# Loading two rows of the first tile ahead, in four transfers of some of the partitions

## The chip, the cores and the metric

The kernel runs on one core of a Trainium2 chip. The metric is the device time of one execution in microseconds (us); lower is better. Times are the median of several unprofiled runs; one more execution is taken with the hardware profiler, and all durations come from it.

## The reference

```python
def reference(x):                      # x: (32, 512, 2048) float32
    half_dim = x.shape[-1] // 2
    x1, x2 = x[..., :half_dim], x[..., half_dim:]
    silu_x1 = x1 * (1 / (1 + np.exp(-x1)))
    return (silu_x1 * x2).astype(np.float32)      # (32, 512, 1024)
```

Each row of 2048 numbers is cut in two halves; the silu of the first is multiplied with the second. 134.22 MB are read and 67.11 MB are written, so the work is mostly moving data.

## The kernel before

The 16,384 rows are cut into 16 tiles of 1024 rows. A tile lies on 128 partitions with `K = 8` rows on each; these eight rows are neighbours in the memory, so that one partition's share of a tile is one stretch of 64 KB of the input and one of 32 KB of the output. There are two input buffers (`xt0`, `xt1`) and two output buffers (`ot0`, `ot1`), used in turn by even and odd tiles.

Per tile there are four kinds of work. `load(i)` (L64) issues the transfer of the tile into its buffer from SP's queue. `silu(i, a, b)` (L71) computes the silu of the first half of rows a to b on ACT, in place. `mul(i, a, b)` (L79) multiplies with the second half on DVE and writes the output buffer. `store(i, a, b)` (L90) issues the transfer to the output from ACT's queue. The order is written out by hand (`manual_schedule`), the waits follow from what reads and writes which buffer, and `implied` (L57) drops those that another wait already covers.

The order (L93 to L114): SP issues the loads of tiles 0 and 1 at once. Tile 0 is computed in four pieces of two rows (`FIRST`), and stored in five transfers (`OPENING`, L16), each of some of the partitions: every fourth partition's rows 0 and 1; the partitions halfway between these, rows 0 to 3, then 4 to 7; every fourth partition's rows 2 to 7; and the odd partitions with all rows. Then SP issues the load of tile 2. Tiles 1 to 14 are computed whole and stored whole; as soon as a tile's product is done, its input buffer is free and SP issues the load of the tile two further on. Tile 15 is computed and stored in two halves (`LAST`). At the end SP waits for all stores.

SP thus issues 16 transfers, all loads, and ACT 21, all stores (five of tile 0, fourteen whole ones, two halves). A load waits for the product of the tile that used its buffer before; a store for its product; a product also for the store that last read its output buffer.

What each engine of the chip's transfer hardware does is kept in the trace as packet records: one record for each stretch of memory moved by one of the core's 16 DMA engines, with its start, duration and size. In this kernel a load gives each engine eight packets of 64 KB, and a whole store eight of 32 KB. A further record of 4 bytes on each engine ends each transfer.

Of the kernel before, what the change touches and what calls it, by code (L numbers as in the profile page):

```python
# [1 line left out]

# [4 lines left out]


K = 8

FIRST = [(0, 2), (2, 4), (4, 6), (6, 8)]

LAST = [(0, 4), (4, 8)]


OPENING = [  # L16
    (slice(0, None, 4), slice(0, 2)),
    (slice(2, None, 4), slice(0, 4)),
    (slice(2, None, 4), slice(4, None)),
    (slice(0, None, 4), slice(2, None)),  # L20
    (slice(1, None, 2), slice(None)),
]
SYNC = mybir.DependencyInfo(mybir.DependencyClass.Sync, mybir.DependencyReason.DATA)


@with_exitstack
def kernel(
    ctx: ExitStack,
    tc: tile.TileContext,
    x: bass.AP,  # L30
    out: bass.AP,
):
    nc = tc.nc
    P = nc.NUM_PARTITIONS

    x_flat = x.flatten_outer_dims()
    out_flat = out.flatten_outer_dims()
    num_rows, in_cols = x_flat.shape
    half = in_cols // 2
    dt = x_flat.dtype  # L40
    n_tiles = num_rows // (P * K)
    assert n_tiles * P * K == num_rows

    x_view = x_flat.rearrange("(n p k) d -> n p k d", p=P, k=K)
    out_view = out_flat.rearrange("(n p k) d -> n p k d", p=P, k=K)

    in_pool = ctx.enter_context(tc.tile_pool(name="in_pool", bufs=1))
    out_pool = ctx.enter_context(tc.tile_pool(name="out_pool", bufs=1))
    xts = [in_pool.tile([P, K, in_cols], dt, name=f"xt{j}") for j in range(2)]
    ots = [out_pool.tile([P, K, half], dt, name=f"ot{j}") for j in range(2)]  # L50

    ctx.enter_context(tc.manual_schedule())

    dmas = []
    loads, silus, muls = {}, {}, {}

    def implied(ins, others):  # L57

        for other in others:
            tc.declare_no_dep(ins.ins, other.ins, reason="another wait implies it")

    def load(i):  # L64
        ins = nc.sync.dma_start(out=xts[i % 2], in_=x_view[i])  # L65
        dmas.append(ins)
        loads[i] = ins
        if i >= 2:
            implied(ins, [loads[i - 2], *silus[i - 2]])

    def silu(i, a, b):  # L71
        x1 = xts[i % 2][:, a:b, :half]
        ins = nc.scalar.activation(out=x1, in_=x1, func=mybir.ActivationFunctionType.Silu)  # L73
        silus.setdefault(i, []).append(ins)
        if i >= 2:
            implied(ins, [*silus[i - 2], *muls[i - 2]])
        return ins

    def mul(i, a, b):  # L79
        xt = xts[i % 2]  # L80
        ins = nc.vector.tensor_mul(  # L81
            out=ots[i % 2][:, a:b], in0=xt[:, a:b, :half], in1=xt[:, a:b, half:]
        )
        muls.setdefault(i, []).append(ins)
        implied(ins, [loads[i]])
        if i >= 2:
            implied(ins, [loads[i - 2], *silus[i - 2], *muls[i - 2]])
        return ins

    def store(i, a, b):  # L90
        dmas.append(nc.scalar.dma_start(out=out_view[i][:, a:b], in_=ots[i % 2][:, a:b]))

    load(0)  # L93
    load(1)
    for a, b in FIRST:
        silu(0, a, b)
        mul(0, a, b)
    for ps, ks in OPENING:
        dmas.append(nc.scalar.dma_start(out=out_view[0][ps, ks], in_=ots[0][ps, ks]))
    load(2)  # L100

    for i in range(1, n_tiles - 1):
        silu(i, 0, K)
        mul(i, 0, K)
        store(i, 0, K)
        if i + 2 < n_tiles:
            load(i + 2)

    i = n_tiles - 1
    for a, b in LAST:  # L110
        last_silu = silu(i, a, b)
        last_mul = mul(i, a, b)
    for a, b in LAST:
        store(i, a, b)  # L114


    for group in ([last_silu], [*dmas[-12:-1], last_mul]):
        seen = nc.sync.nop()
        for ins in group:
            tc.add_manual_dep(seen.ins, ins.ins.name, SYNC, reason="the closing waits")  # L120


# [1 line left out]
_INS = ['x']  # L124
_OUTS = [((32, 512, 1024), 'float32')]


# [23 lines left out]
```

## Time and profile before

| what | value |
|---|---|
| median of three unprofiled runs | 470.75 us (470.7 to 471.8) |
| the profiled execution, in all | 472.5 us |
| its span, first to last recorded work | 470.6 us |
| DVE busy | 139.4 us, 20 instructions |
| ACT busy | 114.1 us, 21 instructions |
| read and written | 134.22 MB and 67.11 MB |
| mean rate over the span | 428 GB/s |
| silu of a whole tile, product of a whole tile | 7.03 us, 8.69 us |
| silu and product of two rows of tile 0 | 1.89 us, 2.29 us |
| a load, from its issue to its landing (median) | 41.9 us |
| a whole store, from its issue to its landing (median) | 49.2 us |

The chain of waits is read backwards from the last instruction: at each step it goes to what released the work. It alternates here between products and transfers. A load and a store of two tiles are under way at most times, so the time from issue to landing holds the wait behind earlier packets on the same 16 engines; the rate says how well the engines are used, the landing time doesn't.

This is the opening of the profiled execution in the timeline (start, duration in us, engine, line, operation, count, and in brackets the idle time before and what ended it):

```profile
0.73 115.68 SPq L65 DMA_DIRECT2D xt<-in_x_dram  x6
22.80 5.51 ACT L73 ACTIVATE xt<-xt 128x2048 f32<-128x2048 f32 x3 [20.80 <-DMA xt<-in_x_dram]
24.74 8.90 DVE L81 TENSOR_TENSOR ot<-xt 128x2048 f32<-128x2048 f32 x4 [24.74 <-ACT xt L73]
27.07 0.55 ACTq L99 DMA_DIRECT2D out_dram<-ot  x1
28.22 1.89 ACT L73 ACTIVATE xt<-xt 128x2048 f32<-128x2048 f32 x1
29.27 6.28 ACTq L99 DMA_DIRECT2D out_dram<-ot  x4
```

ACT waits 20.80 us for tile 0, then computes its four silus one after the other; DVE follows a piece behind; the five opening stores are issued from 27.07 to 35.55. A queue's line in this view (SPq, ACTq) gives the time from the first to the last of the merged issues, not work.

### The profile page before, as it was taken

What the parts mean: (1) busy time and instruction counts of PE and PEld (TensorE: products, weight loads), DVE (VectorE), ACT (ScalarE), POOL (GpSimd) and SP (SyncE); (2) the same over time, 40 slices, a digit from 0 to 9 for tenths busy, and PEclk for the clock granted to TensorE, in tenths of its full rate; (3) what the DMA queues carried; (4) which work ended last, traced back from release to release, by engine and by line L of the source; (5) the groups of instructions that cost most, each with busy time, mean ns of one, the idle gap of its engine ahead of it and who ended that gap; (6) DMA issues with size and microseconds to landing.
All of it is one profiled execution on the core that took longest, in us unless ns stands there. A gap on an engine that the chain in (4) does not pass through costs nothing.

```text
span 470.6 us, 169 instructions
## 1 busy us (share of the span) xinstructions
DVE 139.4 (30%) x20; ACT 114.1 (24%) x21; POOL 0.2 (0%) x4
## 2 busy tenths in 40 slices
DVE  0070513307043070420705106061150602507061
ACT  1051405041050501405014050230503205032060
POOL 0000000000000000000000000000000000000000
DMA  8999899999999999999999999999999999999997
GB/s 357 446 462 422 361 484 407 457 432 401 446 454 437 401 448 421 468 401 446 409 440 443 443 407 485 446 393 415 485 404 446 404 443 446 423 429 482 401 407 315
DMA packets 4880, 201.33 MB, mean 428 GB/s; under 512 B 592, under 2 KB 592, under 8 KB 592
## 3 DMA queue, kind: packets, MB, share of 16 engines
q1 hardware_dynamic: 2304, 134.22, 66.1%
q10 hardware_dynamic: 2576, 67.11, 33.1%
HBM read 134.22 MB, written 67.11 MB: 428 GB/s over the span
## 4 chain that ended last, share of the span: by engine, by line
DMA 80%; DVE 14%; ACT 2%; DVEq 1%; issue 0%; SPq 0%
DMA out_dram<-ot 62%; DMA xt<-in_x_dram 18%; DVE ot L81 14%; ACT xt L73 2%; DVEq L146 1%; SPq L65 0%; DVEq L81 0%
## 5 line engine op out<-in xcount | busy, mean ns | idle before, releaser
L81 DVE TENSOR_TENSOR ot<-xt 128x8192 f32<-128x8192 f32 (+2 forms) x20 | 139.4, 6984 | 321.1 <-DMA out_dram<-ot 261.3
L73 ACT ACTIVATE xt<-xt 128x8192 f32<-128x8192 f32 (+2 forms) x20 | 112.8, 5661 | 340.3 <-DMA xt<-in_x_dram 340.3
L73 ACT ACT_TABLE_LOAD x1 | 1.3, 1283 | 0.7 <-PEq L135 0.7
L135 POOL MEMSET const-bfloat16-1.0<- 128x1 bf16 x1 | 0.1, 101 | 0.0
L135 POOL MEMSET const-uint8-127<- 128x1 uint8 x1 | 0.1, 101 | 0.0
L135 POOL MEMSET const-float32-0.0<- 128x1 f32 x1 | 0.1, 98 | 0.2 <-issue 0.2
L135 POOL MEMSET const-float32-1.0<- 128x1 f32 x1 | 0.1, 98 | 0.0
## 6 DMA issues: line engine op xcount, KB each, us to landing
out_dram<-ot ACTq DMA_DIRECT2D x14, 4096.0 KB, 49.2
out_dram<-ot ACTq DMA_DIRECT2D x3, 2048.0 KB, 9.4
out_dram<-ot ACTq DMA_DIRECT2D x2, 512.0 KB, 18.3
out_dram<-ot ACTq DMA_DIRECT2D x1, 768.0 KB, 29.6
xt<-in_x_dram SPq DMA_DIRECT2D x16, 41.9
out_dram<-ot ACTq DMA_DIRECT2D x1, 256.0 KB, 11.0
```

Of the source, the lines that this page charges most:

```text
L73: ins = nc.scalar.activation(out=x1, in_=x1, func=mybir.ActivationFunctionType.Silu)
L81: ins = nc.vector.tensor_mul(out=ots[i % 2][:, a:b], in0=xt[:, a:b, :half], in1=xt[:, a:b, half:])
L135: nc = _bacc.Bacc("TRN2", target_bir_lowering=False, num_devices=1)
L146: with _tile.TileContext(nc) as tc:
```

## The change

Tile 0 is no longer loaded in one transfer. `load` walks a list, `ARRIVING`, when `i == 0`: rows 6 and 7 come first, in four transfers of 16, 16, 32 and 64 partitions (every 8th from 0; every 8th from 4, halfway between; every 4th from 2; the odd ones); then rows 0 to 5 of all 128 partitions in one. All five go out from SP ahead of the load of tile 1. The other tiles are loaded as before. `loads[i]` becomes a list, and the calls of `implied` are adapted to it. The first three silus of tile 0 read rows 0 to 5 and depend on the fifth transfer, the last one on the four others too.

```diff
+ARRIVING = [
+    (slice(0, None, 8), slice(6, None)),
+    (slice(4, None, 8), slice(6, None)),
+    (slice(2, None, 4), slice(6, None)),
+    (slice(1, None, 2), slice(6, None)),
+    (slice(None), slice(0, 6)),
+]
...
     def load(i):
-        ins = nc.sync.dma_start(out=xts[i % 2], in_=x_view[i])
-        dmas.append(ins)
-        loads[i] = ins
-        if i >= 2:
-            implied(ins, [loads[i - 2], *silus[i - 2]])
+        for ps, ks in ARRIVING if i == 0 else [(slice(None), slice(None))]:
+            ins = nc.sync.dma_start(out=xts[i % 2][ps, ks], in_=x_view[i][ps, ks])
+            dmas.append(ins)
+            loads.setdefault(i, []).append(ins)
+            if i >= 2:
+                implied(ins, [*loads[i - 2], *silus[i - 2]])
...
-        implied(ins, [loads[i]])
+        implied(ins, loads[i])
         if i >= 2:
-            implied(ins, [loads[i - 2], *silus[i - 2], *muls[i - 2]])
+            implied(ins, [*loads[i - 2], *silus[i - 2], *muls[i - 2]])
```

A count of the instructions in their order on each engine shows SP with 20 transfers instead of 16 (16x4096 twice, 32x4096, 64x4096, 128x12288, then the whole tiles), and all else in the same order. The eight completion counters that the transfers share in turn are dealt out differently, which adds waits on SP: ahead of the load of tile 2 for the second small transfer, and ahead of the load of tile 4 for the other four parts of tile 0 and for one opening store.

## The prediction

> **What bounds the kernel now.** I read the page's traffic first, then its chain of waits, then the windows view by stage, then the packet records of the trace.
>
> ```profile
> DVE 139.4 (30%) x20; ACT 114.1 (24%) x21; POOL 0.2 (0%) x4
> ...
> HBM read 134.22 MB, written 67.11 MB: 428 GB/s over the span
> ...
> DMA 80%; DVE 14%; ACT 2%; DVEq 1%; issue 0%; SPq 0%
> ```
>
> DVE works 139 us and ACT 114 us of 470.6, so neither sets the end; the chain gives 80% to transfers. The question is how near the 16 DMA engines are to their own limit, and where they fall short of it. The windows (stretch, DVE, ACT and POOL busy, clock, then the DMA share and GB/s, which count a packet where it begins):
>
> ```profile
> 1.73:2.09 0.36, 0.00 (x0) 0.28 (x1) 0.00 (x0) 1.00 7.60 2549
> 2.09:2.45 0.36, 0.00 (x0) 0.00 (x0) 0.00 (x0) 1.00 0.00 0
> 2.45:2.80 0.35, 0.00 (x0) 0.00 (x0) 0.00 (x0) 1.00 0.94 374
> 11.20:28.90 17.70, 4.16 (x2) 6.10 (x4) 0.00 (x0) 1.00 0.96 415
> 28.90:60.90 32.00, 13.43 (x4) 8.24 (x2) 0.00 (x0) 1.00 1.01 424
> 60.90:118.90 58.00, 17.38 (x2) 14.06 (x2) 0.00 (x0) 1.00 1.00 434
> 118.90:176.90 58.00, 17.38 (x2) 14.06 (x2) 0.00 (x0) 1.00 1.00 434
> 176.90:466.90 290.00, 86.99 (x11) 70.39 (x11) 0.00 (x0) 1.00 1.00 433
> 466.20:467.40 1.20, 0.00 (x0) 0.00 (x0) 0.00 (x0) 1.00 0.96 410
> 467.40:468.20 0.80, 0.00 (x0) 0.00 (x0) 0.00 (x0) 1.00 0.06 21
> 468.20:469.50 1.30, 0.00 (x0) 0.00 (x0) 0.00 (x0) 1.00 0.06 25
> ```
>
> From 61 us on the rate is flat at 433 to 434 GB/s with all engines busy. In the packet records each 64 KB packet there takes 2.418 us, and the next begins 2.414 us after it: 65,536 B / 2.414 us x 16 = 434 GB/s. Pure transfer is therefore 201.33 MB / 434 GB/s = 463.9 us, and the span holds only 6.7 us more. Those lie at the two ends. At the start, 2549 GB/s x 0.36 us is 14 packets of 64 KB, and the other two engines' first packets (374 x 0.35 = 2 packets) begin 0.4 to 1.0 us later. At the end, the last three rows hold about 16 KB begun in 0.8 us and 32 KB in 1.3 us: one engine alone is still working. By the packet records fifteen engines end at 467.4 to 467.7 us and one at 469.5: a lag of 1.8 us that the whole kernel waits for.
>
> The same records tell when that lag arises. The odd engine is the one that begins last, at 2.75 us. Against the latest of the others it is 0.28 us behind after its first packet (5.52 against 5.24), still 0.28 when tile 0 has landed (22.43 against 22.15), 0.67 at 41.3, and 1.78 at 61.0; from there on it keeps pace exactly. So it is not a slower engine: its lag is made in the opening, and since no engine is ever idle again, nothing takes it back.
>
> **The change, part by part.** The profiled execution took 472.5 us in all, its span 470.6; the unprofiled runs have their median at 470.75. I work in changes of the span and put them on the median.
>
> *Packets and completions.* Each engine now moves tile 0 in 1+1+2+4 packets of 16 KB and 8 of 48 KB, 16 instead of 8. In the last stores 16 KB packets begin 0.607 us apart, four of them 2.428 against 2.414 for 64 KB: 5 ns a packet, so 8 x 5 = 0.04 us. Each transfer also ends with a 4-byte completion record of 9 ns on each engine: 4 x 9 = 0.04. Together +0.08 us, on the path, as the engines are never idle.
>
> *Issue on SP.* Four more transfers go out ahead of both big loads. A load's issue takes 0.33 to 0.43 us; ACT's issues of every second or fourth partition 0.48 to 0.68. At 0.55 each the fifth issue starts at 0.73 + 4 x 0.55 = 2.9 us and the second tile's at 3.4. An engine's first packet came 1.0 us after the issue (2.0 on the odd engine), so the fifth transfer is ready by 4.9. The eight small packets keep an engine busy to 1.74 + 0.6 (what its first packet took beyond 2.4) + 8 x 0.607 = 7.2 us: cover 2.3 us, price nothing. If that cover failed, each restart would cost the 0.6 us seen on the first packet, 4 x 0.6 = 2.4.
>
> *Compute of tile 0.* The first silu now waits for the fifth transfer, which is the last of the tile as before; the fourth takes four more waits, long fulfilled, some 17 ns each on ACT. That is hidden behind DVE, whose four products take 2.29 each against 1.89 for the silus. What is late next would be the load of tile 2, queued on SP behind the fourth product and issued at 33.67. The tile 1 packets ahead of it run to about 43.4, so the opening's compute has 43.4 - 33.7 - 1.0 = 8.7 us to spare. New waits ahead of SP's loads of tiles 2 and 4 are for transfers landed tens of us earlier; behind them only later loads are queued. Zero.
>
> *The start of the odd engine.* No row shows a transfer with one packet per engine issued to idle queues. If the late beginning comes from handing out 128 rows, a first transfer of 16 rows removes it, and with it the 0.28 us left after the first packet; the most it could bring is the 0.77 to 1.0 us by which the engine starts behind the fourteen. If it belongs to the engine, it brings 0. The other bound is each small transfer restarting like the first one, 0.6 each. I take -0.28: the start's scatter is nearest to hand-out, since the same engine keeps full pace from 61 us on.
>
> *What the lag grows by.* Between 28.9 and 55 us, while the opening stores go out, 64 KB packets take longer than 2.418 us: on a typical one of the fifteen by 0.13 + 0.34 + 0.07 + 0.20 + 0.25 = 1.0 us, on the odd one by 0.21 + 0.49 + 0.34 + 0.51 + 0.45 + 0.30 = 2.3. The two 0.5 us ones are loads that run while the others store. In step with the others it should stretch as they do, and the lag grew by 1.78 - 0.28 = 1.5: I take -1.5. Bounds: -1.5, and +1.5 if new scatter puts another engine as far behind again.
>
> Sum: 0.08 - 0.28 - 1.5 = -1.7 us; 470.75 - 1.7 = **469.05 us** (case A).
>
> [...]
>
> **The rivals.** B: the lag stays. The first packet already absorbs most of the late start (1.0 us at its beginning, 0.28 at its end), and the rest is made by the opening stores, which the change leaves alone. Then only the 0.08 us is added: 470.85. For it: another engine that began 0.77 us late had caught up after one packet. Against: the engine that fell back is the one that started last.
>
> C, the other side: transfers of some of the partitions disturb the stream by themselves. The stretching lies just where the five such stores run, and nowhere after; at the ends of the first three, the next 64 KB packet took about 0.34, 0.20 and 0.25 us longer on the fifteen, up to 0.5 on the odd one. Four such loads at 0.4 are +1.6, the old lag stays, +0.08: 472.4. It decides from about 0.35 us per transfer. Against it: the last two of the five stores, and the boundary between the first two loads, show no stretch.
>
> [...]
>
> **How the numbers follow.** A difference under 0.3%, 1.4 us, is about what a measurement of this kernel can't tell from none: faster is below 469.3, slower above 472.2. Chances: A 0.40 (468.5 to 470.0; 0.35 of it clear of the bound), B 0.24, C 0.20, D 0.16. Faster: 0.35 from A and 0.02 from B. Same: 0.05 from A, 0.19 from B, 0.03 from C, 0.06 from D = 0.33. Slower: 0.03 from B, 0.17 from C, 0.10 from D = 0.30. The range reaches from A's low end (all of the lag and some of the first packet's 0.6) past C: 468.5 to 472.6. A's own is 468.5 to 470.0.
>
> **What would show it.** Right: first packets of all 16 engines within 0.4 us, the last rows of the windows empty after 467.7, the opening row (28.90 to 60.90) nearer 434 GB/s, silu 0 starting within 0.5 us of 22.8. Wrong: one or more engines ending alone as before (B); longer packets before 12 us (C, D: in D about 1.2 us for 16 KB in the first two transfers); a gap in the packets of an engine between 2 and 8 us (the cover on SP failed).

## The result, and the profile after

The changed kernel takes 472.75 us (median of 7 runs, 472.39 to 473.14), the kernel before 470.77 (7 runs, 470.70 to 472.11): ratio 1.0036, 95% interval 1.0026 to 1.0046. It is slower by 2.0 us, where 1.7 us faster was forecast; the time lies just above the range.

The runs come with their spans, and these put the base right. In the comparisons below, where every run is listed with its span, the kernel before was run 79 times. 59 of these runs have a span of at most 469.1 us (mostly 468.8) and a time about 1.9 us above it; 20 have spans of 469.3 to 471.2. The first profile, with its span of 470.6 and 472.5 us in all, was one of the long executions. The changed kernel's profile has a span of 471.0 and 472.75 us in all, its usual time. So the fair comparison is 468.8 with 471.0, not 470.6 with 471.0.

The page of the changed kernel, traffic and the chain's shares by engine:

```profile
HBM read 134.22 MB, written 67.11 MB: 427 GB/s over the span
...
DMA 80%; DVE 14%; ACT 2%; DVEq 1%; SPq 1%; issue 0%
```

Nothing new bounds the kernel; the rate is 1 GB/s lower. Its windows, in the columns of the prediction:

```profile
1.73:2.09 0.36, 0.00 (x0) 0.28 (x1) 0.00 (x0) 1.00 0.00 0
2.09:2.81 0.72, 0.00 (x0) 0.00 (x0) 0.00 (x0) 1.00 1.29 364
2.81:5.66 2.85, 0.00 (x0) 0.00 (x0) 0.00 (x0) 1.00 0.89 270
5.66:8.26 2.60, 0.00 (x0) 0.00 (x0) 0.00 (x0) 1.00 1.17 460
28.90:60.90 32.00, 13.59 (x4) 9.64 (x3) 0.00 (x0) 1.00 1.00 420
60.90:118.90 58.00, 18.63 (x3) 14.06 (x2) 0.00 (x0) 1.00 0.99 428
118.90:176.90 58.00, 17.39 (x2) 14.06 (x2) 0.00 (x0) 1.00 1.00 434
...
467.40:468.20 0.80, 0.00 (x0) 0.00 (x0) 0.00 (x0) 1.00 0.86 369
468.20:469.50 1.30, 0.00 (x0) 0.00 (x0) 0.00 (x0) 1.00 0.30 126
```

No packet begins in the first row, where 14 began before. From 2.8 to 5.7 us the rate is 270 GB/s, far below the steady 434. The steady rate itself is untouched; the 428 from 60.9 to 118.9 comes from counting a packet where it begins, since by the packet records no more time is lost there than before (0.06 us). At the end many engines, not one, are still at work after 467.4.

Its timeline of the opening:

```profile
24.20 5.51 ACT L83 ACTIVATE xt<-xt 128x2048 f32<-128x2048 f32 x3 [22.19 <-DMA xt<-in_x_dram]
26.14 8.90 DVE L91 TENSOR_TENSOR ot<-xt 128x2048 f32<-128x2048 f32 x4 [26.14 <-ACT xt L83]
28.46 0.55 ACTq L109 DMA_DIRECT2D out_dram<-ot  x1
```

Tile 0 has landed 1.4 us later (24.20 against 22.80). From here the opening runs as before.

The packet records give a measure that the rest of this text uses: the transfer time lost by a moment, that is, the time since the span's start less the bytes moved by then over 434.3 GB/s (64 KB in 2.414 us on each of the 16 engines), a mean over the engines. All entries are worked out from packet records, and the times in the last column are medians. The profile of before is one of the long executions; its late engine adds 0.1 us to the mean by 60 us:

| kernel | first packets, mean us | lost by 12 us | by 25 | by 60 | engines end, us | time, us |
|---|---|---|---|---|---|---|
| before (first profile) | 1.96 | 2.61 | 2.62 | 3.60 | 467.37 to 467.70, one 469.49 | 470.77 |
| changed | 2.27 | 3.79 | 3.91 | 4.79 | 468.39 to 469.64 | 472.75 |
| rows ahead, all partitions | 1.91 | 2.48 | 2.49 | 3.01 | 467.33 to 467.65 | 470.70 |
| rows ahead, two halves | 2.25 | 2.88 | 2.89 | 3.56 | 467.64 to 467.90 | 471.00 |
| no every-8th | 2.20 | 3.53 | 3.58 | 4.03 | 467.71 to 468.88 | 471.68 |
| small ones reversed | 2.30 | 4.14 | 4.18 | 4.24 | 468.00 to 468.56 | 471.83 |
| subsets with all rows | 2.32 | 7.13 | 7.83 | 7.90 | 471.71 to 472.27 | 475.41 |

The change loses 1.2 us by 12 us and nothing more in the mean later: by 60 us it is still 1.2 behind (1.3 against the fifteen engines of before that are not late). Its first packets begin 0.31 us later in the mean; the packets of the first eight rounds are together 1.34 us over their nominal time, where the first 64 KB packet before was 0.65 over; the remaining 0.18 are gaps and completion records. The engines then end 0.3 us apart without the late engine before, and 1.25 apart after, so the last of them, which sets the time, comes at 469.64 instead of 467.70: 1.94 us, the whole difference in time.

### The profile page after: what moved, and what is told of

Its sections match the earlier page's. It is cut to its first block, busy times and chain, and to the rows that moved or that the text cites. A ratio compares the mean times of both kernels' runs of the same rounds, so it can differ in the third digit from the quotient of the medians.

```text
span 471.0 us, 179 instructions
## 1 busy us (share of the span) xinstructions
DVE 139.4 (30%) x20; ACT 114.1 (24%) x21; POOL 0.2 (0%) x4
## 4 chain that ended last, share of the span: by engine, by line
DMA 80%; DVE 14%; ACT 2%; DVEq 1%; SPq 1%; issue 0%
DMA out_dram<-ot 62%; DMA xt<-in_x_dram 18%; DVE ot L91 14%; ACT xt L83 2%; DVEq L156 1%; SPq L75 1%; DVEq L91 0%
## 6 DMA issues: line engine op xcount, KB each, us to landing
out_dram<-ot ACTq DMA_DIRECT2D x1, 768.0 KB, 29.8
```

## The experiments

**The kernel before, once more.** No edit.

> The kernel before, unchanged, profiled and timed once more. Theory (the first profile of before was not its usual execution: it took 472.5 us where its runs have 470.7, and the 1.8 us are the one late engine): most runs 470.7 with a span of 468.9, all 16 engines ending together; a few runs at 471.8 to 472.1. Rival (the profiler adds 1.8 us and the late engine is always there): spans of 470.6 in every run, and again one engine that ends 1.8 us after the others.

Times from 470.63 to 472.94 (12 runs), ratio to its own other runs 1.0011 (0.9996 to 1.0025). The profile taken fell on a long execution again, 472.65 us with a span of 470.7:

```profile
467.40:468.20 0.80, 0.00 (x0) 0.00 (x0) 0.00 (x0) 1.00 0.05 21
468.20:469.50 1.30, 0.00 (x0) 0.00 (x0) 0.00 (x0) 1.00 0.06 25
```

The same two rows as in the first profile: one engine at work alone. The shorter runs have spans of 468.7 to 469.0, 1.7 to 2.0 less, about the length of that lag. So the theory holds for the spans. That no engine is late in the usual execution of this kernel is an inference from the spans; no profile of one was taken.

The packet records of this profile also say which engine is late, and it is not the one that begins last. The late engine begins at 1.84 us, eighth of the sixteen; its first packet is the longest (3.71 us), so it comes out of it last, at 5.55, 0.16 us behind the next. The engine that begins last, at 2.89, ends at 467.5 with the others. In the first profile one engine was both last to begin and last out of its first packet, so the two could not be told apart there.

**Rows 6 and 7 ahead in one transfer of all partitions.**

```diff
 ARRIVING = [
+    (slice(None), slice(6, None)),
-    (slice(0, None, 8), slice(6, None)),
...
     (slice(None), slice(0, 6)),
```

The question is what costs the 1.2 us that the change loses by 12 us.

> Rows 6 and 7 of all 128 partitions in one transfer, then rows 0 to 5: two transfers instead of five, no subset of the partitions. [...] If it is the 16 KB packets or the late begin of the first packet (2.09 instead of 1.73 us): silu 0 at 23.2 to 24.2 and 471.2 to 472.7.

470.70 us, ratio 0.9996 (0.9985 to 1.0008): no difference from before. Its windows at the start and end:

```profile
1.73:2.29 0.56, 0.00 (x0) 0.28 (x1) 0.00 (x0) 1.00 2.00 468
...
467.40:468.20 0.80, 0.00 (x0) 0.00 (x0) 0.00 (x0) 1.00 0.01 0
468.20:469.50 1.30, 0.00 (x0) 0.00 (x0) 0.00 (x0) 1.00 0.00 0
```

All 16 first packets begin within 0.56 us, as early as before, and all engines end together. Neither 16 KB packets nor the part by rows costs anything: only the first packet is long, the next seven take 0.61 each, but for two second ones of 0.79 and 0.87. So the cost lies in having four transfers, each of some of the partitions; this run alone does not tell their number from their partitions. Nor does the kernel gain: the 0.6 us less that it has lost by 60 us (3.01 against 3.60) are gone by 119 us (3.56 against 3.66).

**Two halves ahead** (even, then odd partitions).

```diff
+    (slice(0, None, 2), slice(6, None)),
-    (slice(0, None, 8), slice(6, None)),
-    (slice(4, None, 8), slice(6, None)),
-    (slice(2, None, 4), slice(6, None)),
     (slice(1, None, 2), slice(6, None)),
```

> Rows 6 and 7 ahead in two transfers of the even and the odd partitions, then rows 0 to 5. What remains here of the loss is the late begin of a transfer of some of the partitions (its issue takes 0.54 to 0.59 us instead of 0.37; first packet at 2.06 instead of 1.73, so 0.25 to 0.3 us in the mean) and what puts the engines out of step. If half rate on 16 rows and the late begin are the whole loss: 471.0. If each boundary of a subset transfer also sets the engines apart as with three of them (0.7 us at the end): 471.7.

471.00 us, ratio 1.0006 (0.9997 to 1.0015). By 25 us the lost time is 0.27 us above before, which is the late begin (2.25 against 1.96) and nothing else; by 60 us nothing of it is left (3.56 against 3.60), by 119 us 0.12 (3.78 against 3.66). Issues of some of the partitions took 0.54 to 0.59 us on SP where the first load took 0.37, and the first packet came at 2.05 instead of 1.73. That was seen in every kernel that begins with such a transfer, and in none that begins with all partitions.

**Without the two transfers of 16 partitions** (every 4th, halfway, odd).

```diff
+    (slice(0, None, 4), slice(6, None)),
-    (slice(0, None, 8), slice(6, None)),
-    (slice(4, None, 8), slice(6, None)),
```

If the loss lies in these two transfers, it goes with them.

> Rows 6 and 7 ahead in three transfers (every 4th, halfway, odd), without the two of 16 partitions. [...] If the engines run dry because SP issues such a transfer only each 0.62 us while the first holds 0.6 us of work: the first now holds 1.2 us, so most of the loss goes too, but packets of 16 KB still take longer than 0.61 us in the first microseconds. If every subset transfer costs 0.3 to 0.4 us by itself (C): three instead of four, 472.3.

471.68 us, ratio 1.0011 (1.0001 to 1.0021); 1.1 us below the changed kernel in the medians. The first four packets run at 0.61 to 0.63 us after the fill, so every 4th partition has the full rate. Then, from 5 to 8 us, another 0.65 us are lost while the third small transfer, of the odd partitions, is moved, which was not foreseen. They lie in its packets, which are longer by 0.28 us in the mean in its first round and by 0.26 in its third and fourth, and in gaps of 0.1 ahead of it. The transfer of the odd partitions behind the even ones (two halves) shows none of this, so it is not the partitions; what it is stays open.

**The subsets with all eight rows.**

```diff
-    (slice(0, None, 8), slice(6, None)),
+    (slice(0, None, 8), slice(None)),
...
-    (slice(None), slice(0, 6)),
```

> Tile 0 in four transfers of every 8th, halfway, every 4th and odd partitions with all eight rows: 64 KB packets, no part by rows. [...] Engines running dry between small issues: 2.4 us of work in the first transfer cover SP's next issue, so no loss beyond the begin: silu 0 at 22.8 to 23.4 plus 1.3 us in which ACT loads its table after the landing (off the path), time 470.8 to 471.3. A price on each subset transfer (C): 472.4.

475.41 us, ratio 1.0088 (1.0070 to 1.0106).

```profile
2.05:11.40 9.35, 0.00 (x0) 0.00 (x0) 0.00 (x0) 1.00 1.04 224
11.40:17.10 5.70, 0.00 (x0) 0.00 (x0) 0.00 (x0) 1.00 0.96 368
17.10:26.80 9.70, 0.00 (x0) 0.00 (x0) 0.00 (x0) 1.00 1.00 432
```

The first row holds the two transfers of 16 partitions: 224 GB/s with all engines busy. Their packets of 64 KB took 4.7 us (the first with the fill) and 4.94, against 2.42 in the third row. With large packets, which cover SP's issues (2.4 us of work in the first transfer at the full rate), the two transfers run at half rate: +4.7 us.

**The four small ones in reverse.** The odd partitions first, the two of 16 last.

```diff
+    (slice(1, None, 2), slice(6, None)),
+    (slice(2, None, 4), slice(6, None)),
+    (slice(4, None, 8), slice(6, None)),
     (slice(0, None, 8), slice(6, None)),
-    (slice(4, None, 8), slice(6, None)),
-    (slice(2, None, 4), slice(6, None)),
-    (slice(1, None, 2), slice(6, None)),
```

> The same five transfers, the four small ones in reverse: odd partitions, every 4th, then the two of 16 partitions, then rows 0 to 5. The first transfer now holds 2.4 us of work per engine, so SP's next issues (0.6 us each) are covered and no engine runs dry. If the loss after the first packet is engines running dry: it goes, and only the late begin stays, as with two halves: 471.0. If it is half rate on the two transfers of 16 partitions: 2 x 0.61 us more on every engine in mid-stream, with the late begin 0.3: silu 0 at 24.0 to 24.4 and 472.3 to 472.9.

471.83 us, ratio 1.0019 (1.0010 to 1.0028).

```profile
2.05:6.20 4.15, 0.00 (x0) 0.00 (x0) 0.00 (x0) 1.00 1.02 383
6.20:10.50 4.30, 0.00 (x0) 0.00 (x0) 0.00 (x0) 1.00 1.00 301
10.50:17.70 7.20, 0.00 (x0) 0.00 (x0) 0.00 (x0) 1.00 1.01 437
```

The loss sits in the second row, at the two transfers of 16: the lost time goes from 2.86 at 6 us to 4.14 at 12, 1.28 us, which is 2 x 0.61 and a little. Silu 0 starts at 24.24, as expected for half rate. The time is 0.5 below the 472.3 expected with it, since the opening stores, which cost 1.0 us before, cost 0.06 here. So running dry is not needed for the loss, and the order of the small ones is worth 0.9 us by itself: in reverse, the engines end 0.56 apart, in the order of the change 1.25.

**The small ones behind rows 0 to 5.**

```diff
+    (slice(None), slice(0, 6)),
     (slice(0, None, 8), slice(6, None)),
...
-    (slice(None), slice(0, 6)),
```

> The same five transfers, but rows 0 to 5 first and the four small ones behind them. If the loss belongs to small transfers on idle engines (late begin, fill, engines running dry): it goes, 470.7 to 470.9. [...] If every subset transfer costs 0.3 to 0.4 us: 472.0 to 472.4, with the longer packets behind all four.

482.34 us, ratio 1.0239 (1.0217 to 1.0260): far above what was expected. The packets behind the 16-partition transfers' begin are longer by 0.25 + 0.49 + 0.43 = 1.17 us, so half rate is there in mid-stream too. But the time is lost elsewhere, in the steady tiles:

```profile
60.90:118.90 58.00, 17.91 (x3) 14.06 (x2) 0.00 (x0) 1.00 1.00 423
118.90:176.90 58.00, 16.75 (x2) 14.06 (x2) 0.00 (x0) 1.00 1.00 423
176.90:466.90 290.00, 82.45 (x11) 70.39 (x11) 0.00 (x0) 1.00 1.00 423
```

423 instead of 434 GB/s throughout. The list of who waited for whom changes too (us in total, times, longest):

```profile
DVE ot L91 <- ACT xt L83: 332.7, 16, 23.7
```

Before, 13 products waited for the store of their output buffer and 3 for their silu; here all 16 wait for the silu, that is, for the load. That alone does not make the rate: with the opening stores by rows, below, 15 of 16 products wait for their silu and the rate from 119 us on is 433. Nor do the engines run dry, since by the packet records they stand still for 0.1 us in the mean between 130 and 420 us. The load packets themselves are longer: of the 505 that begin between 130 and 246 us, 87 take over 2% more than 2.418 us, up to 3.35, with a mean of 2.51, while the store packets keep their 1.213. Before, no packet there is longer. Each tile then takes 29.8 us in the mean instead of 29.0 between silus. Rows 0 to 5 land first here, tile 0 is computed 4.6 us earlier and its stores go out earlier; that this is what brings the stream into the slower pattern fits, but is not shown.

**The opening stores by rows**, in the kernel before and with rows 6 and 7 of all partitions ahead.

```diff
 OPENING = [
-    (slice(0, None, 4), slice(0, 2)),
...
+    (slice(None), slice(0, 2)),
+    (slice(None), slice(2, 4)),
+    (slice(None), slice(4, 6)),
+    (slice(None), slice(6, None)),
```

> The kernel before with tile 0 stored in four transfers of two rows on all 128 partitions each, in place of the five transfers of some of the partitions. If the 1.0 us by which 64 KB packets stretch between 28.9 and 55 us comes from storing subsets: no such stretch, 469.7. If it comes with any small store: 470.7. If the odd packets are needed to keep the engines together: one or more engines end late, 471 to 473.

> Both whole-partition forms together: rows 6 and 7 of all partitions ahead, and tile 0 stored by rows. Each engine's first packets then lie within 0.3 us of each other. If both effects add up: 469.5 to 469.7; if the opening's stretch is the same in any form: 470.7, with fewer of the runs that one late engine lengthens.

473.09 and 473.33 us, ratios 1.0048 (1.0035 to 1.0060) and 1.0048 (1.0034 to 1.0061). In the first, the time lost between 25 and 60 us fell from 1.0 to 0.4 us. But then:

```profile
60.90:118.90 58.00, 17.38 (x2) 14.06 (x2) 0.00 (x0) 1.00 0.98 410
118.90:176.90 58.00, 17.38 (x2) 14.06 (x2) 0.00 (x0) 1.00 1.00 433
```

Between 60 and 119 us 2.7 us are lost: the 0.6 gained are given back several times over. The opening stores of some of the partitions cost something and are worth it. Neither is a better kernel, and the two effects do not add up.

**Probes.** Two further loads of 32 KB a partition into the output buffers before these are first written; in the last two probes the load of tile 1 is cut in two, so that each stands between transfers of all partitions. They ask whether such a transfer is slow by the number of its partitions or by which ones they are. At 434 GB/s the 512 KB of 16 partitions take 1.2 us, at half that rate 2.4, 1.2 more.

```diff
     load(0)
+    for j, ps in enumerate([slice(0, None, 8), slice(0, 106, 7)]):
+        part = x_view[0][ps, 0:4].rearrange("p k (h d) -> p (k h) d", h=2)
+        dmas.append(nc.sync.dma_start(out=ots[j][ps], in_=part))
     load(1)
```

> The kernel before with two further loads of 16 partitions x 32 KB between the loads of tiles 0 and 1, into the output buffers before these are first written: partitions 0, 8, 16 ... 120, then 0, 7, 14 ... 105. Both have 16 rows, one packet per engine, the same size, in mid-stream. [...] Rival (16-row or strided transfers are slow as such): the same duration in both. Time 470.75 + 2.4 + 2.4 at most.

> The same frame with the two strides of the earlier probe, now apart from each other: partitions 0, 8 ... 120, then 0, 7 ... 105. [...] If 16 rows run at half rate as such: 1.2 us for both.

> Two further loads into the output buffers, each between transfers of all 128 partitions: partitions 0 to 15, then 0 to 31, 32 KB each. The tile 1 load is cut in two to stand between them. [...] If transfers of 16 rows run at half rate as such and those of 32 at full rate: 1.2 us more, then nothing.

Their times (485.74 us in two runs, 475.85 and 480.78 in one run each) hold the extra bytes and, in part, a worse steady state, so only the lost time around each probe counts:

| partitions | transfer time lost, us | foreseen by 16 rows as such |
|---|---|---|
| 0, 8 ... 120 | 1.3 | 1.2 |
| 0 to 15 | 3.6 | 1.2 |
| 0 to 31 | 2.1 | 0 |
| 0, 7 ... 105 | 0.8 | 1.2 |

The two strides next to each other lost 2.5 together, which looked like 16 rows as such; apart from each other they differ. The window of partitions 0 to 15 with the first packets behind them reads:

```profile
21.70:27.70 6.00, 0.00 (x0) 3.62 (x3) 0.00 (x0) 1.00 1.00 175
27.70:36.20 8.50, 8.26 (x4) 3.68 (x3) 0.00 (x0) 1.00 1.03 444
```

The number of rows does not set the rate: 16 neighbours lose three times what 16 spread ones lose (3.6 against 1.3 us), and 32 neighbours lose 2.1 us although 32 spread ones (every 4th) lose nothing (16 KB packets of 0.61 to 0.63 us). What sets it is which partitions a transfer touches, and with them which rows it reads; by what rule is not shown. The 512 KB to partitions 0 to 15 took 3.6 us more than their nominal 1.2, so 109 GB/s; the two transfers of every 8th partition with all rows ran at 224 GB/s. The stride of 7, with 0.8 us, lies between no loss and half rate and stays open: all 16 of its packets were longer (1.58 to 2.02 us against 1.21).

## Why the prediction was wrong

*The base failed first.* The step "the profiled execution took 472.5 us in all, its span 470.6; ... I work in changes of the span and put them on the median" was wrong, and with it -0.28 and -1.5, the two terms of the lag. The profile was 1.75 us above the median of the runs, and that was read as what profiling adds; it was the late engine itself. In 59 of 79 runs there is no such span, so the median held nothing to take away. Even a change that cures the lag could thus not gain in the usual time. Nor does the cause hold that the prediction gave it, "the engine that fell back is the one that started last": in the second profile of before the late engine began eighth, and the last to begin (2.89 us) kept up; in four other kernels (the small ones behind, in reverse, the subsets with all rows, the opening stores by rows) the last engine begins at 2.72 to 2.97 and ends within 0.6 us of all others. No single engine is late in the changed kernel either, but that is one profile, and most executions of the kernel before have the short span too.

*The start* was put at -0.28 and measured at +0.31: a transfer of some of the partitions is issued in 0.58 us instead of 0.37 and its first packet comes 1.36 us after the issue began, not 1.0. Two engines still begin 0.3 us after the other fourteen (2.68 and 2.72 us against 2.39 at the latest), with 16 rows as with 128; that handing out rows keeps them back was the author's estimate and is not shown.

*The packets.* The first two transfers were given no price in the sum. D, half rate on both, gave +1.2 and had a chance of 0.16; no trace seen before the change shows such a rate. The runs showed it: 2 x 0.61 us in mid-stream (1.28 with the small ones reversed), and 224 GB/s with all rows. In the order of the change the first eight rounds are together 0.69 longer than the fill of before; how much of that is half rate is not separated, since part of it hides in the fill. The opening stores of every 4th partition in the kernel before, with packets of 8, 16 and 24 KB in 0.309, 0.611 and 0.912 us, ran at the full rate; for every 8th that said nothing.

*The cover on SP* was to hold 2.3 us. The issues came 0.62 us apart and the fifth started at 3.25 instead of 2.9; the total was covered. Yet by the records the engines wait some 0.15 us in the mean, most of it ahead of the third transfer. SP's issue does not explain that: it began at 1.99, so by the 1.36 us of the first transfer its packets were due at 3.35, and no engine was done with its second packet before 3.74. What they wait for is open. Extra packets and records were put at 0.08; gaps and records measured 0.18.

*What no step had* is that the small transfers set all engines out of step: 1.25 us between the first and last at the end, against 0.3. That is 0.6 to 0.7 us of the 2.0, since the last engine sets the time. Half rate is not needed for it, since three small transfers without half rate left 1.17; half rate without gaps left 0.56. What sets the engines apart is not shown further.

*Right* were the steady rate, the compute of tile 0 (hidden) and the new waits (SP waits 1.0 us more for loads in all, long before its next load may go out). The price of C was wrong: two halves ahead lost 0.27 us in the opening, the late begin, and no 0.4 each.

## What to carry to other kernels

Before taking a term off a profile, set the profiled execution's time against the median of the runs (472.5 and 470.75 us here): a difference is either overhead or an event that the usual run doesn't have, and the spans of several runs tell which. The rate of a transfer of a few partitions goes by which partitions it touches and not by how many they are (3.6 us lost by 16 neighbours, 1.3 by 16 spread ones), here with packets of 16 to 64 KB; if a first transfer is to be cut, cut it by rows and keep all partitions (470.70 here against 472.75, though no better than uncut). Where every engine is always busy, what sets them apart in the opening is paid at the end (last engine at 469.64 us here, 1.25 behind the first), and a change in the order of the opening can move the whole steady state (482.34).

## What the hardware showed that was not expected

One engine falls behind by 1.8 and 1.9 us in the two profiles of the kernel before, within the first 60 us, and keeps full pace afterwards; 20 of 79 runs have spans lengthened by 0.5 to 2.4 us. What starts it is open; in both profiles it is the engine that comes last out of its first packet, 0.28 and 0.16 us behind the next. The stretch of 64 KB packets during the opening stores (1.0 us) all but vanishes in three kernels (0.06 to 0.07, with the small transfers reversed, behind, or with all rows) that store the same subsets, so it hangs on how loads and stores meet, not on the stores alone; which meeting it is stays open. And a first issue of every 2nd, 4th or 8th partition holds SP for 0.54 to 0.58 us, where one of all 128 takes 0.37. It is not the number of partitions as such: the probe of partitions 0 to 15 was issued in 0.42, and issues of all 128 behind such strided ones took 0.43 to 0.71.
